# Squared row scale at the adds, sums of squares on ScalarE, and an earlier start of retention's q in a two-layer trunk

## The chip, the cores and the metric

The kernel runs on one core of one Trainium2 chip. The metric is the device time of one execution in microseconds (us). TensorE (PE) multiplies, VectorE (DVE), ScalarE (ACT) and GpSimd (POOL) do the elementwise work, SyncE (SP) issues DMAs. SBUF is the on-chip memory with 128 partitions, and PSUM holds eight banks of 128x512 f32 into which TensorE accumulates.

## The reference, cut to what matters

A sequence of 512 tokens with width 1024 passes through two layers, each a token mixer and a squared-ReLU MLP of hidden width 4096, and then a final norm. All is float32.

```python
def rms_norm(x, g):                      # over the width of 1024
    return x * lax.rsqrt(jnp.mean(x * x, -1, keepdims=True) + 1e-6) * g

def squared_relu_mlp(h, w_up, w_down):
    u = jax.nn.relu(h @ w_up)            # 1024 -> 4096
    return (u * u) @ w_down              # 4096 -> 1024

h = x
h = h + stick_breaking_attention(rms_norm(h, g_mix[0]), ...)   # 16 heads of 64
h = h + squared_relu_mlp(rms_norm(h, g_mlp[0]), ...)           # "MLP0"
h = h + retention(rms_norm(h, g_mix[1]), ...)                  # 4 heads
h = h + squared_relu_mlp(rms_norm(h, g_mlp[1]), ...)           # "MLP1"
return rms_norm(h, g_final)
```

The row factor r of a norm is positive, one number for each token. So relu(r·z)² = r²·relu(z)², and r² can stand behind the second product of the MLP as well.

## The kernel before, in words

**Layout.** The state h lies transposed, as eight tiles of 128 features by 512 tokens (`h[0]` to `h[7]`). Each operand of a product is split into a rounded part hi (a cast, by ScalarE) and the rest lo (a subtraction, by VectorE), and each product is made of three 128x512 matmuls, hi·hi, hi·lo and lo·hi. A helper records each TensorE instruction behind the one before it, so TensorE runs in the order in which the code is written; a scheduler orders the other engines, by priorities that it draws from the program, and each engine then works through its own list strictly in order. All matmuls have line L79 and all transposes L82, all splits of made operands L109 (hi) and L110 (lo).

**Weights.** `load_w` fetches 128 rows of two k-tiles, casts them (L119) and subtracts in two halves of 128x512 (L122, tile `wlo`).

**Norms.** A `Norm` sums squares of h over the features: ScalarE squares (L221), VectorE adds (`ssum`), `begin` and `end` sum over partitions by 16 narrow matmuls (`ss`), and GpSimd takes the power to r. `broadcast` builds a diagonal of r on VectorE (`diag`, L256) and multiplies it by ones (`rbps`) to have r along the free axis, as `rb`. The gain is multiplied in when x, the split input of the next product, is made from h (`next_x`: xhi on ScalarE, xlo on VectorE).

**MLP.** `mlp_s` makes eight groups of up products (96 matmuls into four banks each; the bank sets are `set_a`, four banks of tag "a", and `set_b`, two of "z" and two of "t"). At a group's end VectorE makes u = max(up, 0)·rb (L586) and ScalarE squares it into U (L587). Each pair of groups gives a chunk of the down product, which is formed with seven block products of 24 matmuls instead of eight (`plan`; sums of blocks are formed in S and B by VectorE, L639 to L650). `prep` splits a block's operands (tiles a and b, each in halves 0 and 1) one product ahead. Up groups of later chunks and down products alternate on TensorE, 9 matmuls by 6, then 18 matmuls of down. Behind each block product `add_up` adds its two banks to hT, the output laid out by tokens (L726; the first touch in MLP0 is a copy by ScalarE, L723). The last of the four chunks has no up group beside it; its plan is X, Z, X, Z, Y, X, V, by the names of their banks, and V is the last product of an MLP.

**Ends.** At the end of MLP0 hT is transposed back, feature tile by feature tile (`back`, bank `dT`), added to h (L274), and split into x, and retention starts: `side_by_side` makes the first head's q in two banks, x4 to x7 first. At the end of MLP1 the final norm follows: VectorE takes statistics of hT (`stats`, L775; L794 to L797), multiplies the right half by the gain (`scaled`, L779), GpSimd takes the power (L799), ScalarE scales the right half (L801) and VectorE the left (L804), and both halves go out by DMA. Rows 0 and 1 are worked off behind the Y product, rows 2 and 3 behind X and V. The core of it is

```python
for b in blocks:                      # tokens_out(0, 1) after Y, tokens_out(2, 3) after V
    ...
    nc.vector.bn_aggr(mv, sums[b].rearrange("p j s -> p (j s)"))
    ...
    nc.gpsimd.tensor_tensor(r, ms, mhalf[:, 0:1], op=ALU.pow)
    ...
    nc.scalar.activation(o, o, AF.Copy, scale=r)
    ...
    nc.vector.scalar_tensor_tensor(o, o, r, gf[0][:, left], op0=ALU.mult, op1=ALU.mult)
```

Of the kernel before, what the change touches and what calls it, by code (L numbers as in the profile page):

```python
# [12 lines left out]
P = 128  # L13
D = 1024
# [10 lines left out]
def trunk_kernel(  # L25
# [86 lines left out]
    def load_w(src, a, b, name, home=None, sub=None):  # L112

        pool, bufs = home or (wp, 3)
        raw = wp.tile([P, a, b], F32, tag="raw", name=f"raw_{name}", bufs=3)
        nc.sync.dma_start(raw, src)
        hi = pool.tile([P, a, b], F32R, tag="whi", name=f"whi_{name}", bufs=bufs)
        lo = pool.tile([P, a, b], F32R, tag="wlo", name=f"wlo_{name}", bufs=bufs)
        nc.scalar.copy(hi, raw)  # L119
        for j in range(min(a, 2)):  # L120
            ks = slice(j * a // 2, (j + 1) * a // 2) if a > 1 else slice(0, 1)
            (sub or nc.vector).tensor_tensor(  # L122
                lo[:, ks, :], raw[:, ks, :], hi[:, ks, :].bitcast(F32), op=ALU.subtract
            )
        return hi, lo
# [137 lines left out]
    def next_x(k, g, norm):  # L263

        gk = gain[:, g, k : k + 1]
        xhi, xlo = x[k]
        nc.scalar.activation(xhi, h[k], AF.Copy, scale=gk)
        nc.vector.scalar_tensor_tensor(
            xlo, h[k], gk, xhi.bitcast(F32), op0=ALU.mult, op1=ALU.subtract
        )  # L270
        norm.add(k)
# [265 lines left out]
    def mlp_s(layer, norm, finish=None):  # L537
# [13 lines left out]
        with ExitStack() as st:  # L551
            mp = st.enter_context(tc.tile_pool(name=f"mlp{layer}", bufs=2, reuse_waits="tile"))
            hT = mp.tile([P, NB, D], F32, name="hT", bufs=1)
            rb = None
# [10 lines left out]
            def up_steps(g, tags):  # L565

                nonlocal rb
# [16 lines left out]
                for m in range(4):  # L584
                    u = mp.tile([P, S], F32, tag="u", name=f"u{layer}_{g}_{m}")
                    nc.vector.scalar_tensor_tensor(u, banks[m], 0.0, rb, op0=ALU.max, op1=ALU.mult)  # L586
                    nc.scalar.activation(U[:, m, :], u, AF.Square)  # L587
# [128 lines left out]
            def add_up(acc, blocks):  # L716
                for half, cols, sign in blocks:
                    new = finish and (half, cols.start) not in begun
                    begun.add((half, cols.start))
                    for b in range(2):  # L720
                        at = hT[:, 2 * half + b, cols]
                        if new:
                            nc.scalar.activation(at, acc[b], AF.Copy, scale=float(sign))  # L723
                        else:
                            op = ALU.add if sign > 0 else ALU.subtract
                            nc.vector.tensor_tensor(at, at, acc[b], op=op)  # L726

            def down_steps(c):
                ch, banks = chunks[c], {}
                ending = c == CH - 1  # L730
                tags = {"X": "z", "Z": "t", "Y": "a" if ending else "t", "V": "a"}
                order = last_order if ending else range(7)
                for at, (name, blocks) in enumerate(last_plan if ending else plan):
# [20 lines left out]
            def behind(n):

                if finish:
                    back(4 + n, "zt"[n % 2])
                elif n == 0:
                    for b in (2, 3):
                        stats(b, 1)  # L760
                        scaled(b, 1)

            def back(d, tag):
                t = bank(f"dT{layer}_{d}", tag)
# [3 lines left out]
                finish(d)  # L768

            sums = {}  # L770

            def stats(b, j):
                if b not in sums:
                    sums[b] = small.tile([P, 2, 6], F32, tag=f"fst{b}", name=f"fst6_{b}", bufs=1)
                nc.vector.bn_stats(sums[b][:, j, :], hT[:, b, (left, right)[j]])  # L775

            def scaled(b, j):
                at = hT[:, b, (left, right)[j]]
                nc.vector.tensor_tensor(at, at, gf[0][:, (left, right)[j]], op=ALU.mult)  # L779

            def tokens_out(*blocks):

                if finish:
                    if blocks[0]:
                        for d in range(4):
                            back(d, "zt"[d % 2])
                    return
                for b in blocks:
                    if b < 2:
                        stats(b, 1)  # L790
                        scaled(b, 1)
                    stats(b, 0)
                    mv = small.tile([P, 2], F32, tag="mv", name=f"fmv_{b}")
                    nc.vector.bn_aggr(mv, sums[b].rearrange("p j s -> p (j s)"))  # L794
                    ms = small.tile([P, 1], F32, tag="ve", name=f"fms_{b}")
                    nc.vector.tensor_tensor(ms, mv[:, 0:1], mv[:, 0:1], op=ALU.mult)
                    nc.vector.scalar_tensor_tensor(ms, mv[:, 1:2], EPS, ms, op0=ALU.add, op1=ALU.add)  # L797
                    r = small.tile([P, 1], F32, tag="rstd", name=f"fr_{b}")
                    nc.gpsimd.tensor_tensor(r, ms, mhalf[:, 0:1], op=ALU.pow)  # L799
                    o = hT[:, b, right]  # L800
                    nc.scalar.activation(o, o, AF.Copy, scale=r)  # L801
                    nc.scalar.dma_start(out[b * P : (b + 1) * P, right], o)
                    o = hT[:, b, left]
                    nc.vector.scalar_tensor_tensor(o, o, r, gf[0][:, left], op0=ALU.mult, op1=ALU.mult)  # L804
                    nc.sync.dma_start(out[b * P : (b + 1) * P, left], o)
# [24 lines left out]
    def ret_layer(norm0, norm1):  # L830
        w = w_ret_in
        with ExitStack() as st:
# [5 lines left out]
            def side_by_side(c0, name):  # L838

                order = (4, 5, 6, 7, 0, 1, 2, 3)  # L840
                o = [bank(f"{name}{j}", "a") for j in (1, 2)]
                ws = [w_cols(w, 0, c0 + j * P, f"{name}{j}_0") for j in range(2)]
                for ks in (order[:4], order[4:6], order[6:]):
                    for j in range(2):
                        for k in ks:
                            whi, wlo = ws[j]
                            yield from mm3_steps(
                                o[j], whi[:, k, :], wlo[:, k, :], *x[k], k == order[0], k == order[-1]
                            )
                return o  # L850
# [97 lines left out]
            for hd in range(RET_HEADS):  # L948
                dec = rp.tile([P, S], F32, tag="dec", name=f"dec{hd}", bufs=1)
                nc.scalar.dma_start(dec, decay[:, hd, :])  # L950
                qs = ahead or Steps(rotated_steps(hd * 256, f"q{hd}"))
                ahead = None
# [9 lines left out]
                k = whole(rotated_steps(D + hd * 256, f"k{hd}"))  # L962
# [110 lines left out]
```

## Time and profile before

| | |
|---|---|
| three runs | median 1355.61 us (1354.31 to 1355.77) |
| the profiled execution | 1354.56 us, span 1352.8 us, granted TensorE clock 0.996 |
| start to 253.5 us | attention; PE busy 248.7 us, DVE 196.8 us |
| 253.5 to 594.6 us | MLP0; PE 335.4 us, DVE 243.3 us, ACT 149.8 us |
| 594.6 to 994.0 us | retention; PE 398.8 us, DVE 223.7 us |
| 994.0 to 1290.0 us | MLP1 with up groups; PE 296.0 us, DVE 197.7 us |
| 1290.0 to 1330.0 us | MLP1, last chunk; PE 38.4 us, DVE 39.8 us |
| 1330.0 us to the end | V, final norm, output; PE 7.7 us, DVE 16.6 us |

Times inside an execution are counted from the start of its span. In a row of the timeline stand start, duration, engine, line, operation, output<-inputs and shapes, then the number of instructions joined in the row, and in brackets the time that the engine was idle before it with what ended that. A row's duration is longer than the distance to the next start, since instructions of one engine overlap a little: two 128x512 matmuls start 0.227 us apart and each lasts 0.39 us.

### The profile page before, as it was taken

The page shows a single profiled execution, that of the slowest core. Times are in us where ns is not written, and L with a number is a line of the kernel's source. Part 1 is how long each engine was busy: PE and PEld are TensorE (multiplying, and loading weights), DVE is VectorE, ACT ScalarE, POOL GpSimd, SP SyncE. Part 2 cuts the span into 40 slices and gives each one's busy share as a digit, 9 for nine tenths or more (in the row PEclk, how much of TensorE's full clock was granted, in tenths as well). Part 3 has the DMA queues.
Part 4 walks back from the last instruction along what each step waited for, and adds up shares of the span by engine and source line. Part 5 has one row for each costly group of instructions (what it writes and reads, how often), then busy time and mean ns, then how long its engine had stood idle before and what let it go on. Part 6 is the DMA issues. An engine that isn't in the chain of part 4 may idle for free.

```text
span 1352.8 us, 16109 instructions
## 1 busy us (share of the span) xinstructions
PE 1324.9 (98%) x6082; PEld 1095.6 (81%) x6082; DVE 917.9 (68%) x1345; ACT 573.2 (42%) x824; POOL 116.5 (9%) x142
## 2 busy tenths in 40 slices
PE   9999999999999999989999999999999999999995
PEld 7888888788888888778888888888888888888874
DVE  5788886846586775986565554555574668667598
ACT  6466654534444443543332322322253344444352
POOL 1000000200111111100000000000110011111110
PEclk9999999999999999999999999999999999999998
DMA  6455442543454455413232232232434344544351
GB/s 205 125 149 124 120 122 79 163 117 94 143 130 133 113 128 162 83 52 109 71 94 86 78 94 86 78 95 77 159 106 125 83 151 110 140 125 110 109 105 67
DMA packets 99086, 152.13 MB, mean 112 GB/s; under 512 B 5952, under 2 KB 42944, under 8 KB 99008
## 3 DMA queue, kind: packets, MB, share of 16 engines
q1 hardware_dynamic: 79648, 98.12, 24.2%
q0 software_dynamic: 17920, 50.34, 15.3%
q10 hardware_dynamic: 1440, 2.64, 0.5%
q8 instruction: 48, 0.79, 0.2%
q14 instruction: 30, 0.25, 0.1%
HBM read 138.49 MB, written 2.10 MB: 104 GB/s over the span
## 4 chain that ended last, share of the span: by engine, by line
PE 51%; DVE 3%; issue 1%; POOL 0%; ACT 0%; DVEq 0%; POOLq 0%
PE up L79 13%; PE rout L79 7%; PE rg L79 6%; PE rv L79 6%; PE X L79 5%; PE k L79 3%; PE Z L79 3%; PE q L79 2%; PE ro L79 2%; PE Y L79 1%; PE rs L79 1%; DVE hT L726 1%; PE yt L82 1%; DVE fst L775 0%; DVE b_1lo L110 0%
## 5 line engine op out<-in xcount | busy, mean ns | idle before, releaser
L79 PE MATMUL up<-xhi,wlo_up 128*128 128x512 f32 x512 | 200.4, 391 | 0.9 <-DVE wlo_up L122 0.9
L79 PE MATMUL up<-xhi,whi_up 128*128 128x512 f32 x512 | 200.6, 392 | 0.0
L79 PE MATMUL up<-xlo,whi_up 128*128 128x512 f32 x512 | 200.3, 391 | 0.0
L602 POOL DMA_DIRECT2D B<-in_w_mlp_down x92 | 82.8, 903 | 562.3 <-DVE b_1lo L110 261.3
L122 DVE TENSOR_TENSOR wlo_up<-raw_up,whi_up 128x512 fp32r<-128x512 f32 x128 | 83.8, 686 | 66.6 <-ACT whi_up L119 66.6
L79 PEld LDWEIGHTS up<-xhi,wlo_up 128*128 128x128 f32 x512 | 96.1, 188 | 22.0 <-DVE wlo_up L122 1.4
L79 PEld LDWEIGHTS up<-xlo,whi_up 128*128 128x128 f32 x512 | 96.7, 189 | 20.8 <-issue 0.5
L79 PEld LDWEIGHTS up<-xhi,whi_up 128*128 128x128 f32 x512 | 96.1, 188 | 19.7
L119 ACT CAST whi_up<-raw_up 128x1024 fp32r<-128x1024 f32 x64 | 67.1, 1049 | 99.0 <-PE up L79 83.7
L110 DVE TENSOR_TENSOR b_0lo<-B,b_0hi 128x1024 fp32r<-128x1024 f32 x56 | 68.4, 1221 | 3.6 <-ACT b_0hi L109 1.2
L110 DVE TENSOR_TENSOR b_1lo<-B,b_1hi 128x1024 fp32r<-128x1024 f32 x56 | 68.3, 1220 | 2.1 <-ACT b_1hi L109 2.1
L587 ACT ACTIVATE U<-u 128x512 f32<-128x512 f32 x64 | 38.8, 628 | 62.6 <-DVE u L586 61.8
L109 ACT CAST b_0hi<-B 128x1024 fp32r<-128x1024 f32 x56 | 58.7, 1048 | 13.5 <-DVE B L644 5.2
L109 ACT CAST b_1hi<-B 128x1024 fp32r<-128x1024 f32 x56 | 58.7, 1048 | 7.9 <-DVE B L644 3.5
L586 DVE SCALAR_TENSOR_TENSOR u<-up,rb_n 128x512 f32<-128x512 f32 x64 | 42.9, 688 | 27.0 <-PE up L79 26.3
L79 PE MATMUL rout<-ylo,whi_rout 128*128 128x512 f32 x128 | 51.0, 399 | 0.0
L79 PE MATMUL rout<-yhi,wlo_rout 128*128 128x512 f32 x128 | 51.0, 398 | 0.0
L79 PE MATMUL q<-xlo,whi_q 128*128 128x512 f32 x128 | 50.8, 397 | 0.0
L79 PE MATMUL q<-xhi,wlo_q 128*128 128x512 f32 x128 | 50.6, 395 | 0.0
L79 PE MATMUL rout<-yhi,whi_rout 128*128 128x512 f32 x128 | 50.5, 395 | 0.0
L79 PE MATMUL k<-xlo,whi_k 128*128 128x512 f32 x128 | 50.4, 394 | 0.0
L79 PE MATMUL q<-xhi,whi_q 128*128 128x512 f32 x128 | 50.2, 392 | 0.0
(290 smaller groups left out, 3254.2 us busy)
## 6 DMA issues: line engine op xcount, KB each, us to landing
B<-in_w_mlp_down POOLq DMA_DIRECT2D x96, 512.0 KB, 5.4
raw_up<-in_w_mlp_up SPq DMA_DIRECT2D x64, 512.0 KB, 3.7
raw_rv<-in_w_ret_in SPq DMA_DIRECT2D x16, 512.0 KB, 3.8
raw_rg<-in_w_ret_in SPq DMA_DIRECT2D x16, 512.0 KB, 3.6
raw_rout<-in_w_ret_out SPq DMA_DIRECT2D x16, 512.0 KB, 3.6
raw_q<-in_w_sb_in SPq DMA_DIRECT2D x8, 512.0 KB, 4.6
raw_k<-in_w_sb_in SPq DMA_DIRECT2D x8, 512.0 KB, 4.0
q<-hi SPq DMA_DIRECT2D x32, 128.0 KB, 3.6
```

Source lines behind the costliest of these rows:

```text
L79: pe(nc.tensor.matmul(o, a, b, start=start, stop=stop, **kw))
L82: pe(nc.tensor.transpose(o, a, ident))
L109: nc.scalar.copy(hi, src_ap)
L110: (eng or nc.vector).tensor_tensor(lo, src_ap, hi.bitcast(F32), op=ALU.subtract)
L119: nc.scalar.copy(hi, raw)
L122: (sub or nc.vector).tensor_tensor(lo[:, ks, :], raw[:, ks, :], hi[:, ks, :].bitcast(F32), op=ALU.subtract)
L586: nc.vector.scalar_tensor_tensor(u, banks[m], 0.0, rb, op0=ALU.max, op1=ALU.mult)
L587: nc.scalar.activation(U[:, m, :], u, AF.Square)
L602: nc.gpsimd.dma_start(t[:, ks, :], src[:, ks, :], **kw)
L726: nc.vector.tensor_tensor(at, at, acc[b], op=op)
```

## The change

The change has six parts.

1. `load_w` subtracts in one operation of 128x1024.
2. The MLPs' norm has no broadcast. r² and −r² are made by two small VectorE operations, `norm.begin` and `norm.end` stand after 48 matmuls of the first group instead of 28, and at a group's end ScalarE takes relu from PSUM to U and then squares U in place. The relus and squares are 64 each over both MLPs.
3. `add_up` multiplies by r² or −r², a number for each partition, while it adds (one VectorE operation as before, of another form; the first touch in MLP0 stays with ScalarE).
4. In the last chunk the banks of X and Z change tags.
5. MLP0's end: V's transposes stand late in V, then 24 matmuls of retention's q on x4 to x7 (`early`) ahead of the transposes of x0 to x3, and the norm's sums behind all of these. In retention the norm and its broadcast stand 20 and 30 matmuls into k.
6. MLP1's end: sums of squares by ScalarE with its accumulator (`squares`), the gain's multiplication by GpSimd (`by_gain`, L807 in the new numbering), two small VectorE operations (L811, L812), the power by GpSimd (L814), and the row multiplications as before (L819, L822).

```diff
-        for j in range(min(a, 2)):
-            ...
+        (sub or nc.vector).tensor_tensor(lo, raw, hi.bitcast(F32), op=ALU.subtract)
...
-                    if g == 0 and n == 28:
+                    if g == 0 and n == 48:
                         norm.begin()
                         r = norm.end()
-                    if g == 0 and n == 52:
-                        rb = norm.broadcast(r)
+                        nc.vector.tensor_tensor(r2[:, 0, :], r, r, op=ALU.mult)
+                        nc.vector.tensor_scalar(r2[:, 1, :], r2[:, 0, :], -1.0, None, op0=ALU.mult)
...
                 for m in range(4):
-                    u = mp.tile([P, S], F32, tag="u", name=f"u{layer}_{g}_{m}")
-                    nc.vector.scalar_tensor_tensor(u, banks[m], 0.0, rb, op0=ALU.max, op1=ALU.mult)
-                    nc.scalar.activation(U[:, m, :], u, AF.Square)
+                    nc.scalar.activation(U[:, m, :], banks[m], AF.Relu)
+                for m in range(4):
+                    nc.scalar.activation(U[:, m, :], U[:, m, :], AF.Square)
...
-                            op = ALU.add if sign > 0 else ALU.subtract
-                            nc.vector.tensor_tensor(at, at, acc[b], op=op)
+                            nc.vector.scalar_tensor_tensor(at, acc[b], by, at, op0=ALU.mult, op1=ALU.add)
...
-                tags = {"X": "z", "Z": "t", "Y": "a" if ending else "t", "V": "a"}
+                tags = {"X": "t", "Z": "z", "Y": "a", "V": "a"} if ending else {"X": "z", "Z": "t", "Y": "t"}
...
+            def between(at, n):
                 if finish:
-                    back(4 + n, "zt"[n % 2])
+                    if at == 6 and n >= 14 and (n - 14) % 3 == 0:
+                        back(4 + (n - 14) // 3)
+                elif at == 4 and n == 3:       # Y: squares(0, 1), squares(1, 1), by_gain(0), by_gain(1)
+                elif at == 5 and n == 15:      # X: squares(0, 0), squares(1, 0), row_scale(0), row_scale(1)
+                elif at == 6 and n == 3:       # V: squares and by_gain of 2 and 3, rows_out(0), rows_out(1)
...
+            def back_left(acc, blocks):
+                add_up(acc, blocks)
+                early.go(24)
+                for d in x_order[4:]:
+                    back(d)
+                for d in x_order:
+                    nxt.add(d)
...
+            def squares(b, j):
+                junk = mp.tile([P, 512], F32, tag="junk", name=f"junk{b}_{j}", bufs=1)
+                nc.scalar.activation(junk, hT[:, b, (left, right)[j]], AF.Square, accum_out=ssq[:, b, j : j + 1])
+            def by_gain(b):
+                at = hT[:, b, right]
+                nc.gpsimd.tensor_tensor(at, at, gf[0][:, right], op=ALU.mult)
...
+            def last_out(acc, blocks):
+                add_up(acc, blocks, (0,))
+                squares(2, 0)
+                row_scale(2)
+                add_up(acc, blocks, (1,))
+                squares(3, 0)
+                rows_out(2)
+                row_scale(3)
+                rows_out(3)
...
-                    qs.go(40)
+                    qs.go(24)
+                    ks.go(20)
                     norm0.begin()
                     r = norm0.end()
-                    qs.go(7)
+                    ks.go(10)
                     rb = norm0.broadcast(r)
```

VectorE in MLP1's last chunk, from the Y adds to the lo of V's operands. Before (a1_3_6 and b1_3_6 are V's operands, the last digit is the half; gf is the gain, fr the row factor):

```order
L726 TENSOR_TENSOR hT_8218<-hT_8218,Y1_3_1_10623 128x512
L775 BN_STATS fst6_0_10668<-hT_8218 128x6 x2
L779 TENSOR_TENSOR hT_8218<-hT_8218,gf_10618 128x512
L794 BN_AGGR fmv_0_10672<-fst6_0_10668 128x2
L775 BN_STATS fst6_1_10683<-hT_8218 128x6
...
L804 SCALAR_TENSOR_TENSOR hT_8218<-hT_8218,fr_0_10677,gf_10618 128x512
...
L110 TENSOR_TENSOR b1_3_6_0lo_10705<-B1_3_00_10380,b1_3_6_0hi_10704 128x1024
...
L804 SCALAR_TENSOR_TENSOR hT_8218<-hT_8218,fr_1_10692,gf_10618 128x512
L110 TENSOR_TENSOR b1_3_6_1lo_10725<-B1_3_00_10380,b1_3_6_1hi_10724 128x1024
```

The same place now:

```order
L110 TENSOR_TENSOR b1_3_4_1lo_10445<-B1_3_01_10169,b1_3_4_1hi_10444 128x1024
L728 SCALAR_TENSOR_TENSOR hT_8073<-Y1_3_0_10408,r2_8074,hT_8073 128x512
L110 TENSOR_TENSOR a1_3_4_1lo_10441<-U1_6_9866,a1_3_4_1hi_10440 128x512
L728 SCALAR_TENSOR_TENSOR hT_8073<-Y1_3_1_10409,r2_8074,hT_8073 128x512
L110 TENSOR_TENSOR a1_3_6_0lo_10463<-U1_7_10153,a1_3_6_0hi_10462 128x512
L110 TENSOR_TENSOR b1_3_6_0lo_10467<-B1_3_00_10166,b1_3_6_0hi_10466 128x1024
L110 TENSOR_TENSOR a1_3_6_1lo_10483<-U1_7_10153,a1_3_6_1hi_10482 128x512
L110 TENSOR_TENSOR b1_3_6_1lo_10487<-B1_3_00_10166,b1_3_6_1hi_10486 128x1024
L811 TENSOR_TENSOR fms_0_10496<-ssq1_8075 128x1
```

The statistics, the gain and the row multiplications of rows 0 and 1 no longer stand between the Y adds and V's operands; the row multiplications now follow the X adds.

GpSimd at the same place, now (before there are only the four powers behind the last DMA):

```order
L603 DMA B1_3_00_10166<-in_w_mlp_down 128x2x512 x2
L807 TENSOR_TENSOR hT_8073<-hT_8073,gf_10404 128x512 x2
L814 TENSOR_TENSOR fr_0_10499<-fms_0_10496,mhalf_74 128x1
L814 TENSOR_TENSOR fr_1_10504<-fms_1_10501,mhalf_74 128x1
L807 TENSOR_TENSOR hT_8073<-hT_8073,gf_10404 128x512 x2
L814 TENSOR_TENSOR fr_2_10564<-fms_2_10561,mhalf_74 128x1
L814 TENSOR_TENSOR fr_3_10576<-fms_3_10573,mhalf_74 128x1
```

Four multiplications by the gain have come to GpSimd, behind its last DMA.

TensorE in V at the end of MLP0, before:

```order
L79 MATMUL V_3_0_5048<-b_3_6_0hi,a_3_6_0hi 128x512
L82 MATMUL dT_4_5054<-ident,hT 128x128 x4
L79 MATMUL V_3_0_5048<-b_3_6_0lo,a_3_6_0hi 128x512
...
L82 MATMUL dT_7_5103<-ident,hT 128x128 x4
L79 MATMUL V_3_1_5049<-b_3_6_1lo,a_3_6_1hi 128x512
L79 MATMUL V_3_1_5049<-b_3_6_1hi,a_3_6_1lo 128x512
L82 MATMUL dT_0_5118<-ident,hT 128x128 x4
```

and now:

```order
L79 MATMUL V_3_1_4968<-b_3_6_0hi,a_3_6_0lo 128x512
L82 MATMUL dT_4_4984<-ident,hT 128x128 x4
...
L79 MATMUL V_3_1_4968<-b_3_6_1hi,a_3_6_1lo 128x512
L82 MATMUL dT_7_5017<-ident,hT 128x128 x4
L79 MATMUL q_5027<-xhi_94,whi_q_0_5031 128x512
L79 MATMUL q_5027<-xlo_95,whi_q_0_5031 128x512
L79 MATMUL q_5027<-xhi_94,wlo_q_0_5032 128x512
L79 MATMUL q_5027<-xhi_96,whi_q_0_5031 128x512
```

The transposes of x4 to x7 stood after 4, 10, 16 and 22 of V's 24 matmuls and stand after 15, 18, 21 and 24, and q's first matmuls come directly behind them.

VectorE at that place, now (h4 and xlo4 belong to x4, and so on):

```order
L273 TENSOR_TENSOR h4_82<-dT0_4_4984,h4_82 128x512
L120 TENSOR_TENSOR wlo_k01_0_5156<-raw_k01_0_5153,whi_k01_0_5155 128x1024
L264 SCALAR_TENSOR_TENSOR xlo4_95<-h4_82,gain_71,xhi4_94 128x512
L273 TENSOR_TENSOR h5_83<-dT0_5_4995,h5_83 128x512
L273 TENSOR_TENSOR h6_84<-dT0_6_5006,h6_84 128x512
L273 TENSOR_TENSOR h7_85<-dT0_7_5017,h7_85 128x512
L264 SCALAR_TENSOR_TENSOR xlo5_97<-h5_83,gain_71,xhi5_96 128x512
```

The whole lo of a weight and the adds of h6 and h7 stand between the adds of h4 and h5 and the lo of x5.

More of the change, by code (lines that the diff above doesn't have):

```diff
@@ L261, in broadcast, with scaled_x @@
             return rb
[L263 removed]
+    def scaled_x(k, g):
         gk = gain[:, g, k : k + 1]
@@ L270, in next_x @@
         )
+    def next_x(k, g, norm):
+        scaled_x(k, g)
         norm.add(k)
@@ L714, in mlp_s, with add_up @@
             begun = set()
-            def add_up(acc, blocks):
+            def add_up(acc, blocks, only=(0, 1)):
                 for half, cols, sign in blocks:
                     new = finish and (half, cols.start) not in begun
-                    begun.add((half, cols.start))
-                    for b in range(2):
-                        at = hT[:, 2 * half + b, cols]
+                    if only[-1] == 1:
+                        begun.add((half, cols.start))
+                    for b in only:
+                        t = 2 * half + b
+                        at, by = hT[:, t, cols], r2[:, int(sign < 0), t : t + 1]
                         if new:
-                            nc.scalar.activation(at, acc[b], AF.Copy, scale=float(sign))
+                            nc.scalar.activation(at, acc[b], AF.Copy, scale=by)
                         else:
-                            op = ALU.add if sign > 0 else ALU.subtract
-                            nc.vector.tensor_tensor(at, at, acc[b], op=op)
+                            nc.vector.scalar_tensor_tensor(at, acc[b], by, at, op0=ALU.mult, op1=ALU.add)
             def down_steps(c):
@@ L767, in back @@
                 residual(d, t)
[L768 to L805, printed above, removed]
@@ new lines, in rows_out @@
+            def rows_out(b):
+                rows, r = slice(b * P, (b + 1) * P), scales[b]
+                o = hT[:, b, left]
+                nc.vector.scalar_tensor_tensor(o, o, r, gf[0][:, left], op0=ALU.mult, op1=ALU.mult)
+                nc.sync.dma_start(out[rows, left], o)
+                o = hT[:, b, right]
+                nc.scalar.activation(o, o, AF.Copy, scale=r)
+                nc.scalar.dma_start(out[rows, right], o)
+            def last_out(acc, blocks):
[7 more added lines that the diff above has]
+                rows_out(3)
@@ L827, in mlp_s, with side_by_side, ret_layer @@
                 dn.end()
-    def ret_layer(norm0, norm1):
+    x_order = (4, 5, 6, 7, 0, 1, 2, 3)
+    def side_by_side():
+        o = [bank(f"q0{j}", "a") for j in (1, 2)]
+        ws = [w_cols(w_ret_in, 0, j * P, f"q0{j}_0") for j in range(2)]
+        for ks in (x_order[:4], x_order[4:6], x_order[6:]):
+            for j in range(2):
+                for k in ks:
+                    whi, wlo = ws[j]
+                    yield from mm3_steps(
+                        o[j], whi[:, k, :], wlo[:, k, :], *x[k], k == x_order[0], k == x_order[-1]
+                    )
+        return o
+    def ret_layer(norm0, norm1, early):
         w = w_ret_in
@@ L836, in ret_layer @@
             crs = rp.tile([P, 2, S], F32, name="crs", bufs=1)
[L838 to L850, printed above, removed]
             def rotated_steps(c0, name):
                 if name == "q0":
-                    t1, t2 = yield from side_by_side(c0, name)
+                    while not early.done:
+                        early.go(1)
+                        yield
+                    t1, t2 = early.value
                 else:
@@ L961, in ret_layer @@
                 q = qs.end()
-                k = whole(rotated_steps(D + hd * 256, f"k{hd}"))
+                k = ks.end()
                 v = values(hd, group(w, 2 * D + hd * RV, KT, x, f"rv{hd}", set_b, token_major=True))
```

59 lines of the change are left out of this document (39 added, 20 removed).

## The prediction

> **What bounds the kernel.** I read the page's busy times first, then what TensorE waited for, then the places of the longest waits on the timeline.
>
> ```profile
> span 1352.8 us, 16109 instructions
> PE 1324.9 (98%) x6082; PEld 1095.6 (81%) x6082; DVE 917.9 (68%) x1345; ACT 573.2 (42%) x824; POOL 116.5 (9%) x142
> ```
>
> TensorE is busy for 1324.9 of 1352.8 us, so work taken from other engines is worth nothing unless TensorE waits for it. Gains can come from matmuls removed, from the 28 us of gaps, and from the tail. The waits of TensorE (total, times, longest):
>
> ```profile
> PE V L79 <- DVE b_0lo L110: 4.8, 1, 4.8
> PE dT L82 <- DVE hT L726: 3.2, 2, 2.5
> PE X L79 <- DVE hT L726: 2.1, 2, 1.1
> PE X L79 <- DVE b_1lo L110: 1.1, 2, 0.6
> PE up L79 <- DVE wlo_up L122: 0.9, 1, 0.9
> ```
>
> All lie at the ends of the MLPs or the start of one, the largest in front of V in MLP1. Matmuls there, and a table by stretches (length, busy PE, PEld, DVE, ACT, POOL, then the granted clock):
>
> ```profile
> 1330.10 0.39 PE L79 MATMUL V<-b_0hi,a_0hi 128*128 128x512 f32 x1
> 1335.33 0.80 PE L79 MATMUL V<-b_0lo,a_0hi 128*128 128x512 f32 x1 [4.84 <-DVE b_0lo L110]
> 1300.00:1310.00 10.00, 10.00 (x46) 8.14 (x45) 10.00 (x14) 4.58 (x6) 2.44 (x2) 1.00 0.34 55
> 1335.00:1338.00 3.00, 2.67 (x6) 1.82 (x6) 2.56 (x5) 0.72 (x1) 0.87 (x1) 0.54 0.22 83
> ```
>
> V's second matmul waits 4.84 us, and after that pause the clock is 0.54 for a while. In the last chunk VectorE is full (10.00 of 10.00) and as late as TensorE. VectorE's list there:
>
> ```profile
> 1295.60 1.27 DVE L726 TENSOR_TENSOR hT<-hT,X 128x512 f32<-128x512 f32 x2
> 1296.79 0.69 DVE L110 TENSOR_TENSOR a_0lo<-S,a_0hi 128x512 fp32r<-128x512 f32 x1
> 1297.39 1.22 DVE L110 TENSOR_TENSOR b_0lo<-B,b_0hi 128x1024 fp32r<-128x1024 f32 x1
> 1298.53 0.68 DVE L639 TENSOR_TENSOR S<-U,U 128x512 f32<-128x512 f32 x1
> ...
> 1306.29 1.23 DVE L110 TENSOR_TENSOR b_0lo<-B,b_0hi 128x1024 fp32r<-128x1024 f32 x1
> ...
> 1327.12 1.28 DVE L726 TENSOR_TENSOR hT<-hT,Y 128x512 f32<-128x512 f32 x2
> 1328.32 1.28 DVE L775 BATCH_NORM_STATS2 fst<-hT 128x6 f32<-128x512 f32 x2
> ...
> 1334.06 1.22 DVE L110 TENSOR_TENSOR b_0lo<-B,b_0hi 128x1024 fp32r<-128x1024 f32 x1
> ...
> 1336.39 0.75 DVE L804 SCALAR_TENSOR_TENSOR hT<-hT,fr,gf 128x512 f32<-128x512 f32 x1 [0.44 <-POOL fr L799]
> 1337.06 1.22 DVE L110 TENSOR_TENSOR b_1lo<-B,b_1hi 128x1024 fp32r<-128x1024 f32 x1
> ...
> 1346.67 1.42 DVE L804 SCALAR_TENSOR_TENSOR hT<-hT,fr,gf 128x512 f32<-128x512 f32 x2 [0.59 <-POOL fr L799]
> ```
>
> From start to start an add or a subtraction of 128x512 takes 0.60 us (1296.79 to 1297.39), one of 128x1024 1.14 us (to 1298.53), and the form with a number for each partition 0.67 us (1336.39 to 1337.06). From 1328.32 to the lo of V's operand stands the norm of rows 0 and 1. The last VectorE operation ends at 1348.09, and 4.7 us of output follow.
>
> **The parts and their costs.** The sum is made against the profiled execution, 1354.56 us; the median of the runs is 1.05 us above it.
>
> Broadcast in the MLPs. The chain of waits has, in MLP1,
>
> ```profile
> 1012.77 0.86 PE rbps_n L79 x2
> ```
>
> It is TensorE's own work in a stretch without gaps, and it goes in both MLPs: −1.7 us. The norm's sums only move, and r² isn't wanted before the first add.
>
> Relu and square. Per group VectorE loses four u of 0.67 us, and ScalarE has eight operations instead of four.
>
> ```profile
> L587 ACT ACTIVATE U<-u 128x512 f32<-128x512 f32 x64 | 38.8, 628 | 62.6 <-DVE u L586 61.8
> 1289.52 0.40 PE L79 MATMUL up<-xhi,wlo_up 128*128 128x512 f32 x1
> ```
>
> At 0.6 us each, with the two casts that its new list has between them, the four relus are through about 1.9 us after the last up matmul (1289.52), and the banks are wanted after 24 matmuls of down, 24 × 0.227 = 5.4 us. ScalarE waited 61.8 us for u in all. I take 0; bounds 0 and +1.4 (0.1 us at each of 14 group ends, should a cast come late). VectorE's relief is covered by TensorE everywhere but in the last chunk.
>
> Whole lo of a weight. Only at the start of MLP0 does TensorE wait for one:
>
> ```profile
> 254.27 1.28 DVE L122 TENSOR_TENSOR wlo_up<-raw_up,whi_up 128x512 fp32r<-128x512 f32 x2
> 255.01 0.50 PE L79 MATMUL up<-xhi,wlo_up 128*128 128x512 f32 x1 [0.92 <-DVE wlo_up L122]
> ```
>
> The first half was enough there; now the whole is waited for, 1.14 − 0.60 = +0.5 us. Elsewhere weights come ahead and the 0.5 us are hidden.
>
> Last chunk up to V. Against VectorE's list before I go through the new one: two u leave (−1.3 us), but one U subtraction comes earlier (+0.6), S waits for the last two squares (about +0.6), and adds cost 0.07 us more each (eleven, +0.8). So VectorE has the lo of the third product's first operand at about 1307.8 instead of 1307.4, TensorE, which starts the chunk 1.1 us sooner because X has free banks (half of the 2.1 us above), waits 1.3 and 1.0 us in the third product, and V starts at about 1330.5 instead of 1330.1: +0.4 us in MLP1 and, with both U subtractions and a weight's lo in the list, +0.7 us in MLP0. Bounds −1.1 (banks alone) to +2.
>
> V and the tail of MLP1. With these lengths the new list, which has no gap from the third product on, reaches the end of the Y adds at 1328.3, as before. With the norm of rows 0 and 1 out of the way, the lo of V's first half follows directly: 1328.3 + 0.60 + 1.14 = 1330.0, so V does not wait, and the lo of the second half is there at 1331.8, where V wants it. V ends 24 × 0.227 later, at 1336.2 instead of 1342.7, at full clock. VectorE: X adds to 1334.7, two row multiplications to 1336.0, V adds to 1337.4. Then the chain of the last rows, by these groups:
>
> ```profile
> L221 ACT ACTIVATE sq_n<-h 128x512 f32<-128x512 f32 x28 | 17.3, 617 | 0.0
> L799 POOL TENSOR_TENSOR fr<-fms,mhalf 128x1 f32<-128x1 f32 x4 | 2.8, 704 | 31.8 <-DVE fms L797 31.8
> ```
>
> The square by ScalarE, behind a row scale in its queue, ends at 1337.9; then come two small operations (0.3), the power (0.7), a row multiplication (0.67), and the same small chain for row 3, which stands behind that multiplication: 1341.5 against 1348.1, −6.6 us.
>
> But four multiplications by the gain now run on GpSimd beside it, of which before shows the like only in the attention:
>
> ```profile
> 194.77 1.60 POOL L110 TENSOR_TENSOR o<-oF,o 128x512 fp32r<-128x512 f32 x1 [13.05 <-ACT o L109]
> 195.40 1.52 DVE L423 TENSOR_TENSOR sg<-sg,keep 128x511 f32<-128x511 f32 x1
> L110 POOL TENSOR_TENSOR o<-oF,o 128x512 fp32r<-128x512 f32 x7 | 9.7, 1388 | 176.4 <-ACT o L109 176.4
> ```
>
> A VectorE operation with both inputs in SBUF, which takes 0.68 us alone, took 1.52 us beside it: +0.84. The first two multiplications fall on the casts b of X and V (two SBUF inputs), the third on the row multiplications, the fourth on V adds, whose one input is in PSUM. Three by 0.84 = 2.5 us, of which 0.4 lie in the wait for ScalarE: gain 6.6 − 2.1 = −4.5 us. Bounds −6.6 (none counts) and −3.1 (1.30 each). I take 0.84, since it is the price that a row shows.
>
> The Trainium skill, *SBUF — State Buffer*, section *Who interferes with whom*, says that such a pair contends for one shared port pair, which whoever issues first holds for its whole instruction; the trace agrees as far as the VectorE operation of 195.40 ends 0.55 us after GpSimd's does (194.77 + 1.60 = 196.37). Where GpSimd comes first from the start, the price by this rule is a whole GpSimd operation.
>
> End of MLP0 and start of retention. TensorE from V's start to the first matmul of rv:
>
> ```profile
> 581.99 0.39 PE L79 MATMUL V<-b_0hi,a_0hi 128*128 128x512 f32 x1
> 585.61 0.66 PE L82 MATMUL dT<-ident,hT 128*128 128x128 f32 x4 [2.54 <-DVE hT L726]
> 593.19 1.64 PE L82 MATMUL dT<-ident,hT 128*128 128x128 f32 x13 [0.65 <-DVE hT L726]
> 608.00 1.10 PE L79 MATMUL rbps_n<-diag_n,ones 128*128 128x512 f32 x2 [0.63 <-DVE diag_n L256]
> 620.05 0.39 PE L79 MATMUL rv<-whi_rv,xhi 128*128 128x512 f32 x1
> ```
>
> Of 38.1 us 3.8 are waits (2.54 + 0.65 + 0.63); the rest, the same matmuls, stays. The first wait shrinks to some 0.3, as the transposes come 11 × 0.227 = 2.5 us later; the second goes, as 24 matmuls (5.4 us) stand between V and dT0; the third goes, as ten matmuls (2.3 us) instead of seven stand in front of the broadcast. What is late next is x. Between the add of h4 and the lo of x5 VectorE has 1.14 + 0.67 + 3 × 0.60 us, and q wants x5 three matmuls after x4: about 1.4 us of wait, 0.3 more for x6, and for x0 to x3, whose adds, casts and lo start with dT0, about 1.3. Sum 3.3: −0.5 us; bounds −3.8 (x in time) and +1.5.
>
> Sum: −1.7 + 0.5 + 0.7 − 0.5 − 4.5 = −5.5 (the +0.4 of MLP1 stands in the tail's times). That is 1349.1 us in the frame of the profiled execution and 1350.1 from the median. A profiled execution need not lie as far under the median the next time; I take the middle, **1349.6 us**.
>
> **Rivals.** (1) GpSimd's multiplications cost VectorE nothing: the last operation ends at 1341.5, 2.1 us more are gained, 1347.5 us. For it: most rows of GpSimd (mean 1388 ns) ran beside VectorE without a trace of it; against it the row of 195.40.
> (2) Each of the three costs a whole operation of 1.30 us: 3 × 0.46 = 1.4 us less, 1351.0 us. For it, VectorE's list is unbroken there, so a GpSimd operation that gets in is in front of a whole VectorE operation. By the rule of the Trainium skill above (*SBUF — State Buffer*, *Who interferes with whom*) this price is the one paid.
> (3) x is in time in retention: 3.3 us more, 1346.3 us. The long list between h4 and x5 speaks against it.
> (4) The change does not do in the tail what it says: V waits as long as before, now for a cast that ScalarE makes late, because its list has two squares between the casts of X's and V's operands. Then only −1.7 + 0.5 remain with small terms, 1354.5 us, no change. For it, a square with accumulator has no row; one would have to cost 2 us more than the 0.6 us of a plain one.
> (5) Slower: ScalarE at the ends of the groups. If the eight operations and the casts behind them made TensorE wait there, with 14 ends in two MLPs, it would decide from (5.5 + 2.7)/14 = 0.6 us each. At 0.9 us each it gives 1349.6 + 12.6 = 1362 us. Against it, the 3.5 us between relus done and banks wanted.
>
> **How the numbers follow.** Chances: forecast 0.40, (1) 0.20, (2) 0.16, (3) 0.06, (4) 0.12, (5) 0.06. About 0.2% (2.7 us) is what a measurement can tell from no change, so faster begins under 1352.9: forecast, (1), (2) and (3), 0.82. Same is (4), 0.12; slower is (5), 0.06. The range leaves out (4) and (5), 0.18 in all, and takes in the ends of the other terms: 1345.2 below (rival 3 and no lost start), 1353.0 above (rival 2 with +2 in the last chunk).
>
> **What would show it.** Right: no rbps in the MLPs; V in MLP1 at 0.23 us a matmul with waits under 1 us; last VectorE operation at 1342 to 1345 on the clock of before less the 1 to 2 us gained earlier; casts b of 128x1024 that take about 2 us beside GpSimd's multiplications; a wait of about 1 us for xlo in q. Wrong: a wait for up banks at groups' ends, V still waiting 3 us or more, or TensorE waits of several us in the last chunk, which VectorE's list, counted here by hand, would then have caused.

## The result: 0.5% faster, and the profile after

| | before | changed |
|---|---|---|
| runs, median | 1355.69 us (1354.31 to 1356.12, 4 runs) | 1348.28 us (1348.08 to 1350.28, 4 runs) |
| the profiled execution, its span | 1354.56, 1352.8 us | 1350.28, 1348.5 us |

The ratio is 0.995, 95% interval 0.9933 to 0.9968. Forecast were 1349.6 us. The page's first lines of the changed kernel:

```profile
span 1348.5 us, 15871 instructions
PE 1325.7 (98%) x6078; PEld 1093.8 (81%) x6078; DVE 867.5 (64%) x1121; ACT 607.8 (45%) x902; POOL 124.5 (9%) x146
```

VectorE lost 50 us of work and ScalarE gained 35; TensorE is as busy as before. What TensorE waits for now (total, times, longest), the small waits in the attention left out:

```profile
PE X L79 <- DVE hT L728: 1.8, 3, 0.6
PE X L79 <- DVE b_0lo L110: 1.5, 2, 0.8
PE q L79 <- DVE xlo L264: 1.5, 3, 0.6
PE up L79 <- DVE wlo_up L120: 1.5, 1, 1.5
...
PE X L79 <- DVE b_1lo L110: 1.1, 2, 0.5
...
PE X L79 <- ACT b_0hi L109: 0.6, 1, 0.6
...
PE q L79 <- ACT xhi L263: 0.2, 1, 0.2
```

The 4.8 us in front of V are gone, and so are the waits of the transposes, of the broadcast, and of X for its banks at the start of the last chunks. In their place stand q's waits for x, a longer one for the first weight's lo, and three of X for its banks in the mixed stretches, where the kernel before has none. V and the end, on TensorE, VectorE, GpSimd and ScalarE:

```profile
1331.55 0.39 PE L79 MATMUL V<-b_0hi,a_0hi 128*128 128x512 f32 x1
1337.39 0.39 PE L79 MATMUL V<-b_1hi,a_1lo 128*128 128x512 f32 x1
1326.01 1.22 DVE L110 TENSOR_TENSOR b_1lo<-B,b_1hi 128x1024 fp32r<-128x1024 f32 x1
1327.91 1.03 DVE L110 TENSOR_TENSOR a_1lo<-U,a_1hi 128x512 fp32r<-128x512 f32 x1
1329.53 1.13 DVE L110 TENSOR_TENSOR a_0lo<-U,a_0hi 128x512 fp32r<-128x512 f32 x1
1336.35 1.02 DVE L819 SCALAR_TENSOR_TENSOR hT<-hT,fr,gf 128x512 f32<-128x512 f32 x1
1337.30 1.76 DVE L819 SCALAR_TENSOR_TENSOR hT<-hT,fr,gf 128x512 f32<-128x512 f32 x1
1343.31 0.75 DVE L819 SCALAR_TENSOR_TENSOR hT<-hT,fr,gf 128x512 f32<-128x512 f32 x1 [0.72 <-POOL fr L814]
1323.95 4.44 POOL L807 TENSOR_TENSOR hT<-hT,gf 128x512 f32<-128x512 f32 x1 [10.14 <-ACT junk L801]
1328.36 1.74 POOL L807 TENSOR_TENSOR hT<-hT,gf 128x512 f32<-128x512 f32 x1
1335.54 1.28 POOL L807 TENSOR_TENSOR hT<-hT,gf 128x512 f32<-128x512 f32 x1
1336.79 1.72 POOL L807 TENSOR_TENSOR hT<-hT,gf 128x512 f32<-128x512 f32 x1
1339.75 0.63 ACT L801 ACTIVATE junk<-hT 128x512 f32<-128x512 f32 x1 [2.72 <-DVE hT L728]
1340.29 0.19 ACT L801 ACTIVATION_READ_ACCUMULATOR junk<-hT 128x1 f32 x1
```

V's 24 matmuls start within 5.84 us instead of 12.16. The four multiplications by the gain take GpSimd 4.44, 1.74, 1.28 and 1.72 us. On VectorE the subtractions of 128x1024 (lo of b) still take 1.22 us beside the first of them; two of 128x512 (lo of a) take 1.03 and 1.13 instead of 0.68, and two row multiplications 1.02 and 1.76 where two took 1.42 together. Each of these four longer operations ends 0.55 to 0.56 us after a GpSimd multiplication ends (1328.39, 1330.10, 1336.82 and 1338.51).

To say where the time went, I cut both profiled executions at TensorE's first and last instructions of each stage (us):

| stretch of TensorE | before | changed | difference |
|---|---|---|---|
| start to first up of MLP0 | 253.46 | 255.43 | +1.97 |
| first up to first X: MLP0; MLP1 | 49.54; 52.20 | 49.20; 51.28 | −0.34; −0.92 |
| first X to last up (mixed): MLP0; MLP1 | 238.39; 238.39 | 237.95; 238.87 | −0.44; +0.48 |
| last up to V (last chunk): MLP0; MLP1 | 40.60; 40.58 | 41.32; 40.72 | +0.72; +0.14 |
| V of MLP0 to first rv | 38.06 | 36.97 | −1.09 |
| rv to first up of MLP1 | 378.88 | 379.81 | +0.93 |
| V of MLP1, its starts; from there to the end | 12.16; 10.54 | 5.84; 11.11 | −6.32; +0.57 |

The sum is −4.3, the difference of the spans. The 1.97 us at the start are no part of the change: in that execution the first matmuls ran slowly, in others of the same program text there (the kernel without GpSimd's multiplications, below) not. A row of the changed kernel:

```profile
6.96 0.63 PE L79 MATMUL v<-whi_v,xlo 128*128 128x512 f32 x1
```

and the same matmul of that kernel:

```profile
6.41 0.40 PE L79 MATMUL v<-whi_v,xlo 128*128 128x512 f32 x1
```

The profiled execution of the changed kernel is 2.0 us above its median, that of before 1.1 below: −4.3 − 2.0 − 1.1 = −7.4, the difference of the medians.

### The profile page after: what moved, and what is told of

It is laid out like the page before. It is cut to its first block, busy times and chain, and to the rows that moved or that the text cites. A ratio compares the mean times of both kernels' runs of the same rounds, so it can differ in the third digit from the quotient of the medians.

```text
span 1348.5 us, 15871 instructions
## 1 busy us (share of the span) xinstructions
PE 1325.7 (98%) x6078; PEld 1093.8 (81%) x6078; DVE 867.5 (64%) x1121; ACT 607.8 (45%) x902; POOL 124.5 (9%) x146
## 4 chain that ended last, share of the span: by engine, by line
PE 91%; DVE 6%; issue 1%; ACT 1%; DMA 0%; POOLq 0%; POOL 0%; DVEq 0%
PE up L79 25%; PE X L79 9%; PE rout L79 7%; PE rg L79 7%; PE k L79 6%; PE rv L79 6%; PE q L79 6%; PE Z L79 5%; PE v L79 3%; PE Y L79 3%; PE so L79 3%; PE ro L79 2%; PE z L79 2%; PE av L79 1%; PE t L82 1%
## 5 line engine op out<-in xcount | busy, mean ns | idle before, releaser
L120 DVE TENSOR_TENSOR wlo_up<-raw_up,whi_up 128x1024 fp32r<-128x1024 f32 x64 | 78.1, 1222 | 79.0 <-ACT whi_up L119 79.0
L109 ACT CAST b_0hi<-B 128x1024 fp32r<-128x1024 f32 x56 | 58.7, 1048 | 4.0 <-PE X L79 2.1
L586 ACT ACTIVATE U<-up 128x512 f32<-128x512 f32 x64 | 37.1, 592 | 49.1 <-PE up L79 49.1
L79 PE MATMUL k<-xhi,whi_k 128*128 128x512 f32 x128 | 50.4, 394 | 0.0
L79 PE MATMUL rg<-whi_rg,xhi 128*128 128x512 f32 x128 | 50.2, 392 | 0.0
```

The costliest lines, as they stand in the source:

```text
L79: pe(nc.tensor.matmul(o, a, b, start=start, stop=stop, **kw))
L109: nc.scalar.copy(hi, src_ap)
L120: (sub or nc.vector).tensor_tensor(lo, raw, hi.bitcast(F32), op=ALU.subtract)
L586: nc.scalar.activation(U[:, m, :], banks[m], AF.Relu)
```

## The experiments

They were run in three groups, each beside the kernel before on the same chip: e1, e2, e10 and e6 (median of before 1355.83 us), e16, e11, e13 and e14 (1356.05), and e17 to e20 (1354.78). Ratios are to the kernel before of the same group.

**The tail alone (e1).** In the kernel before, only the final norm is exchanged for the new one:

```diff
-                    if ending and at == 4:
-                        tokens_out(0, 1)
...
+                elif at == 4 and n == 3:       # squares, by_gain, row_scale, rows_out and last_out as in part 6
```

> The kernel before with part 6 alone (the new final norm). Theory T (the gain is made in MLP1's tail, because the final norm's VectorE work leaves the place in front of V's casts and shrinks): V's wait of 4.84 us goes, VectorE ends 4 to 5.5 us earlier, about 1350.5 us. Rival S (the gain is spread, VectorE needs the relief of relu and of whole lo as well): V still waits 2 us or more, 1353 us or later.

Measured: 1357.64 us, ratio 1.0011 (1.0002 to 1.002). Slower, and yet V's wait went as expected:

```profile
PE V L79 <- DVE b_0lo L110: 0.2, 1, 0.2
```

From V's first matmul to the end it takes 16.6 us instead of 22.7. The time was lost where nothing had been changed: each MLP's mixed stretch took 241.28 and 241.27 us instead of 238.39, without a wait.

**The tail undone (e2).** In the changed kernel the old final norm is put back.

```diff
-                elif at == 4 and n == 3:       # and the rest of part 6
                 elif at == 6 and n == 3:
                     for b in (2, 3):
+                        stats(b, 1)
+                        scaled(b, 1)
...
+                    if ending and at == 4 and not finish:
+                        tokens_out(0, 1)
```

> The changed kernel with part 6 undone (final norm as before, parts 1 to 5 kept). T: V waits 4 to 5 us again and some 5.5 us are lost, about 1353.8 us. Rival S: at most 2 us are lost, 1349 to 1350.3 us.

Measured: 1361.92 us, ratio 1.0045 (1.0031 to 1.0059), slower than before. V waits again,

```profile
PE V L79 <- DVE b_0lo L110: 4.3, 1, 4.3
```

and from V to the end it takes 23.9 us instead of the changed kernel's 17.0: 6.9 us, somewhat more than the 5.5 of T. The rest is again in the mixed stretches (242.29 and 242.97 us). Neither theory had a place for that.

**The place of the norm alone (e10).**

```diff
+                        if ending and at == 6 and n == 13:
+                            tokens_out(0, 1)
                         yield
...
-                    if ending and at == 4:
-                        tokens_out(0, 1)
```

> The kernel before with one thing moved: the final norm of rows 0 and 1, still on VectorE, stands in V instead of ahead of it. Theory E (what counts is that VectorE has less to do up to the end): V's wait goes, but the same 13 us of VectorE work stand behind the X adds, the last operation ends at about 1347.5, 1355.1 us. Rival P (what counts is the place alone, V's wait and the clock after it): the whole gain of about 5 us, 1350.7 us.

Measured: 1355.49 us, ratio 0.9996 (0.9987 to 1.0005): E. V is through in 5.58 us, but 16.7 us follow instead of 10.5. With V's wait gone VectorE's list is still there. So it is not enough to take the norm out of V's way; work had to leave VectorE's list. Which of the two that left counts more, the sums of squares or the gain, no run separates.

**Without GpSimd's multiplications (e6).**

```diff
-                nc.gpsimd.tensor_tensor(at, at, gf[0][:, right], op=ALU.mult)
+                pass
```

> The changed kernel with GpSimd's four multiplications by the gain left out: the right half of the output is not multiplied by g_final. Theory L (they hold up VectorE's operations with two SBUF inputs): the two lo of 1.03 and 1.13 us go back to 0.68, the two row multiplications from 2.71 us to 1.42, about 2 us in all on VectorE, of which 1.2 at least on the path, 1346.3 to 1347.1 us. Rival 1 of the prediction (they cost VectorE nothing on the path): 1348.3 us.

Measured: 1346.06 us, ratio to before 0.9929 (0.9917 to 0.9942), 2.2 us under the changed kernel. The same operations on VectorE there:

```profile
1327.18 0.68 DVE L110 TENSOR_TENSOR a_0lo<-U,a_0hi 128x512 fp32r<-128x512 f32 x1
1333.55 1.41 DVE L819 SCALAR_TENSOR_TENSOR hT<-hT,fr,gf 128x512 f32<-128x512 f32 x2
```

L it is, by 0.2 us more than its range. V takes 5.2 us instead of 5.8, and what follows 9.7 instead of 11.1.

**What made e1 and e2 slow? (e16)** The same matmuls took 1.2 to 1.9% longer in a stretch nearly without waits. The compiled programs show what else differs: the new small tiles ssq and r2 take 32 bytes in each partition, and every tile allocated behind them starts elsewhere. In before the tiles of the MLPs (U, B, a, b, S) start at 960 modulo 1024 bytes, in e2 at 992. In e1 they start at 800, since the tiles of the old norm's statistics go as well. In the changed kernel both shifts together give 832, while retention's tiles, which stand ahead of r2 and move with ssq alone, start at 800.

> The kernel before with a tile of 32 bytes that nothing reads put ahead of the others in the pool of small tiles, so that every later tile (norms, attention's, both MLPs', retention's) starts 32 bytes further on; no other instruction changes. Theory A (tiles that start 32 bytes off a multiple of 64 make TensorE's matmuls beside them slower, as the two slow kernels' up and down matmuls of 0.230 us instead of 0.227 suggest): +2.9 us in each MLP and +0.9 us in retention, 1362.5 us or more. Rival N (it was something else in those two kernels): 1355.7 us.

```diff
+    pad = small.tile([P, 8], F32, tag="pad", name="pad", bufs=1)
+    nc.gpsimd.memset(pad, 0.0)
```

Measured: 1363.78 us, ratio 1.006 (1.0048 to 1.0073). So the place of the tiles costs time, as A has it; whether its rule of 64 bytes holds is the next question. The mixed stretch of MLP0 and retention, as the table by windows has them (length, busy PE with its count, PEld, DVE, ACT, POOL, granted clock), of before and of this kernel:

```profile
303.00:541.39 238.39, 238.39 (x1048) 196.91 (x1047) 160.65 (x214) 102.32 (x135) 31.02 (x36) 1.00 0.47 128
620.05:998.93 378.88, 378.88 (x1721) 313.57 (x1720) 207.19 (x356) 115.74 (x150) 12.40 (x21) 1.00 0.31 94
```

```profile
302.93:544.57 241.64, 241.64 (x1048) 196.32 (x1046) 160.95 (x214) 102.17 (x135) 31.00 (x36) 1.00 0.46 127
624.81:1005.17 380.36, 380.36 (x1722) 313.42 (x1720) 207.18 (x356) 115.75 (x150) 12.36 (x21) 1.00 0.30 94
```

The same 1048 matmuls, the same work on the other engines, TensorE busy all the time and the clock at 1.00: 3.25 us longer, for a tile that nothing reads. It isn't only the matmuls that read the moved tiles: two up matmuls, which read x and weights alone, and these lie where they lay, start 0.231 us apart on average in this stretch instead of 0.227.

**The parts with tiles of 64 bytes (e11, e13, e14).** The edits, beside parts of the change (e11 is part 6 alone, e13 parts 2 and 3, e14 the whole change):

```diff
-            ssq = small.tile([P, NB, 2], F32, tag="ssq", name=f"ssq{layer}", bufs=1)
+            ssq = small.tile([P, NB, 4], F32, tag="ssq", name=f"ssq{layer}", bufs=1)
-            r2 = mp.tile([P, 2, NB], F32, name="r2", bufs=1)
+            r2 = mp.tile([P, 4, NB], F32, name="r2", bufs=1)
```

> The kernel before with part 6 alone, as e1_tail_alone, but the new small tile ssq takes 64 bytes instead of 32, so that the tiles behind it start at multiples of 64 again. A: the MLPs run at 0.227 us a matmul, and the tail's gain of about 5 us shows: 1351 us. N: 1357.6 us as without it.

> The kernel before with parts 2 and 3 alone (relu and square on ScalarE, r squared at the adds), the tile r2 taking 64 bytes. A, with the broadcast's 0.86 us gone from each MLP and a last chunk that gains little: 1354.0 to 1354.6 us. Rival S (relief of VectorE is what the change lives on): 1352 us or less.

> The changed kernel with ssq and r2 of 64 bytes each instead of 32 (in the changed kernel the two together leave the MLPs' tiles at multiples of 64, but retention's 32 off). A: retention is 0.9 us shorter, 1347.4 us. N: 1348.3 us.

Measured: 1344.79 us for the tail alone (ratio 0.9919, 0.9906 to 0.9933), 1360.23 for parts 2 and 3 (1.0036, 1.0023 to 1.0049), 1349.88 for the changed kernel (0.9958, 0.9945 to 0.9972). The first was 6 us better than forecast, the second 6 worse, the third 2.5 worse; so a multiple of 64 is not the rule. Their MLP tiles start at 832, 0 and 896 modulo 1024, with mixed stretches of 237.10, 240.69 and 240.91 us in MLP0. Parts 2 and 3 alone can't be judged by their time; but the stretch ahead of the first X, where no such difference was seen, is 0.87 us shorter in MLP0 and 0.91 in MLP1, which is the broadcast.

**Separating the place from the change (e17 to e20).** In the kernel before `pad` as above, with `[P, 224]` (e17) or `[P, 32]` (e18); in the changed kernel (e19, e20) ssq as above and

```diff
-            r2 = mp.tile([P, 2, NB], F32, name="r2", bufs=1)
+            r2 = mp.tile([P, 64, NB], F32, name="r2", bufs=1)
```

> The kernel before with an unused tile of 896 bytes ahead in the pool of small tiles; the tiles of the mixers and MLPs then start at 832 modulo 1024, as in e11_tail_alone_64, instead of 960. Theory A (TensorE's rate in the stages depends on where these tiles lie): 1.3 us less in each MLP, 2.3 less in retention, 0.8 less in attention, 1350.2 us; then part 6 is worth the 5.4 us that are left of the 11.3 of e11. Rival N (e11's gain is part 6's own): 1355.9 us.

> The kernel before with an unused tile of 128 bytes ahead: the tiles start at 64 modulo 1024. Theory M (what counts is the start modulo 128: the quick places so far, 960 and 832, lie 64 off a multiple of 128, as x and the weights do, the slow ones, 992, 800, 896 and 0, do not): as before, 1355 to 1356.5 us. Rival Q (another pattern): 1358 us or more, or 1353.5 or less.

> The changed kernel with ssq of 64 bytes and r2 of 1024 bytes, so that the tiles of all stages start at 832 modulo 1024 (in the changed kernel attention's and retention's start at 800). A: retention 376.6 us instead of 379.8, attention 0.8 less, the MLPs unchanged, 1344.3 us. Rival N: 1348.3 us.

> As e19_after_832, and part 1 undone (lo of weights in two halves) and, in the last norm, the two row factors of a pair made in one operation each and the row multiplications of rows 0 and 1 put behind the V adds. The wait for the first weight's lo falls from 1.5 to 0.9 us; V's adds come 2.5 us earlier, and row 3's factor no longer stands behind row 2's multiplication: the last VectorE operation 2 us earlier; 1341.7 us in all. Rival (the scheduler's order and GpSimd's multiplications eat it): 1344 us.

Measured: 1350.20 us for before with 896 bytes (ratio 0.9965, 0.9953 to 0.9978), 1350.30 with 128 bytes (0.9965, 0.9952 to 0.9977), 1345.14 for the changed kernel at 832 throughout (0.9926, 0.9912 to 0.9939), 1342.18 for the last (0.9903, 0.9889 to 0.9916). The first came out as A had it. In the second M missed and Q holds: 64 is not as 960, it is better, as good as 832. In the third retention came to 376.53 us, as A had it. The windows of e17:

```profile
302.29:539.38 237.09, 237.09 (x1047) 196.39 (x1046) 160.33 (x214) 102.32 (x135) 31.04 (x36) 1.00 0.47 129
619.66:996.20 376.54, 376.54 (x1721) 313.33 (x1720) 207.04 (x356) 115.75 (x149) 12.39 (x21) 1.00 0.30 95
```

| starts modulo 1024: MLPs; retention | program | mixed stretch of MLP0; MLP1 | rv to up |
|---|---|---|---|
| 960; 960 | before | 238.39; 238.39 | 378.88 |
| 992; 992 | before (e16) | 241.64; 241.64 | 380.36 |
| 832; 832 | before (e17) | 237.09; 237.09 | 376.54 |
| 64; 64 | before (e18) | 237.09; 237.09 | 376.56 |
| 800; 800 | part 6 alone (e1) | 241.27; 241.27 | 379.81 |
| 832; 832 | part 6 alone (e11) | 237.09; 237.09 | 376.56 |
| 0; 960 | parts 2 and 3 (e13) | 240.69; 240.88 | 378.89 |
| 992; 960 | changed without part 6 (e2) | 242.29; 242.97 | 378.80 |
| 832; 800 | changed | 237.95; 238.87 | 379.81 |
| 896; 832 | changed (e14) | 240.91; 241.65 | 376.56 |
| 832; 832 | changed (e19) | 237.99; 238.83 | 376.53 |

Each stretch goes by the place of its own stage's tiles: retention takes 378.8 to 378.9 us at 960 in three programs and 376.5 to 376.6 at 832 in four, whatever the MLPs' tiles do.

So at a like place part 6 is worth about 5 us: 5.4 by the medians of e17 and e11 (1350.20 and 1344.79, from two groups whose medians of before lie 1.3 us apart), and 4.7 in the stretches that it touches, since V to the end takes 6.1 us less but the last chunk ahead of V 1.4 us more (42.05 instead of 40.63). Parts 1 to 5 together bring nothing (1344.79 to 1345.14), but they are gains and losses that cancel. From e11 to e19 the broadcasts and the first lo give 1.3 us, the end of MLP0 1.1 and the last chunk of MLP1 1.3, while that of MLP0 loses 1.0 and the mixed stretches 2.6. Of these parts only part 1 is tried by itself, by undoing it in e20, and parts 2 and 3 as a pair in e13; parts 4 and 5 are read from their stretches alone.

The last kernel, e20, is the fastest of all, 6.1 us under the changed one. Its edits beside the place: lo in halves again, and

```diff
+                ms = small.tile([P, 2], F32, tag="ve", name=f"fms_{b}")
+                nc.vector.tensor_tensor(ms, ssq[:, b : b + 2, 0], ssq[:, b : b + 2, 1], op=ALU.add)
...
+                add_up(acc, blocks, (1,))
+                squares(3, 0)
+                row_scale(2)
+                for b in range(NB):
+                    rows_out(b)
```

The 3.0 us against e19 are near the 2.6 forecast, from other places: in the profiled executions the tail from V to the end gives 1.0 us where 2 were expected, and the mixed stretches 1.7 where none was. With the halves the three waits of X for its banks have all but gone. The first of them in e19, and the same place in e20 (L732 is the add there):

```profile
464.68 1.22 DVE L120 TENSOR_TENSOR wlo_up<-raw_up,whi_up 128x1024 fp32r<-128x1024 f32 x1
465.82 1.22 DVE L110 TENSOR_TENSOR b_1lo<-B,b_1hi 128x1024 fp32r<-128x1024 f32 x1
466.95 1.40 DVE L728 SCALAR_TENSOR_TENSOR hT<-X,r,hT 128x512 f32<-128x512 f32 x2
466.87 0.39 PE L79 MATMUL up<-xhi,wlo_up 128*128 128x512 f32 x1
467.85 0.47 PE L79 MATMUL X<-b_0hi,a_0hi 128*128 128x512 f32 x1 [0.59 <-DVE hT L728]
468.15 0.40 PE L79 MATMUL X<-b_0lo,a_0hi 128*128 128x512 f32 x1
```

```profile
463.61 0.68 DVE L122 TENSOR_TENSOR wlo_up<-raw_up,whi_up 128x512 fp32r<-128x512 f32 x1
464.21 1.22 DVE L110 TENSOR_TENSOR b_1lo<-B,b_1hi 128x1024 fp32r<-128x1024 f32 x1
465.34 1.40 DVE L732 SCALAR_TENSOR_TENSOR hT<-X,r,hT 128x512 f32<-128x512 f32 x2
465.79 0.39 PE L79 MATMUL up<-xhi,wlo_up 128*128 128x512 f32 x1
466.23 0.47 PE L79 MATMUL X<-b_0hi,a_0hi 128*128 128x512 f32 x1
466.54 0.39 PE L79 MATMUL X<-b_0lo,a_0hi 128*128 128x512 f32 x1
```

From the up matmul to the second X matmul it takes 1.28 us in e19 and 0.75 in e20, where two starts without a wait take 0.45. The 0.59 of the waits' list leaves out a part of this, since it counts idle time only from the end of the row before. At the end of e20 the row multiplications of rows 2 and 3:

```profile
1334.15 1.41 DVE L821 SCALAR_TENSOR_TENSOR hT<-hT,fr,gf 128x512 f32<-128x512 f32 x2 [0.81 <-POOL fr L815]
```

Rows 2 and 3 now share one wait for their factors.

## Why the prediction was right, and where its terms were off

The forecast was −5.5 us by the parts, and −7.4 were measured. The change also moves tiles, which the prediction did not know: −1.30 in each MLP (960 to 832) and +0.93 in retention (960 to 800), −1.7 us. At a like place (e17 to e19) the change brought −5.1. That this is so near the sum of the parts is in part luck: the mixed stretches lost 2.6 us that had been put at nothing, and the end of MLP0 and the tail together gave about 3 us more than forecast.

- Broadcast and whole lo, −1.7 + 0.5: measured −0.34 − 0.92 = −1.3 in the stretches ahead of X. The wait for the first lo is 1.46 instead of 0.92 us, +0.54.
- Relu and square 0, lo hidden elsewhere: this step failed. At a like place (e17 to e19) the mixed stretches grew by 0.90 and 1.74 us. Of these 2.6 us, 2.5 are the three waits of X for banks whose adds come late (hT, L728): listed with 0.59 us, each costs 0.83 from start to start (1.28 less 0.45 in the rows above). The wrong part is "hidden elsewhere": the whole lo of 1.22 us stands ahead of the adds in VectorE's list, and in halves again (e20) 1.7 of the 2.6 us went. The 0.3 us that are left at each of the three places are not explained. With the 0.5 at the first lo the whole lo lost 2.2 us.
- Last chunk, +0.7 and +0.4: +0.72 and +0.14.
- End of MLP0, −0.5: −1.1 in these executions. Waits of 0.60, 0.23, 0.60 and 0.30 us replaced 3.82; the 3.3 forecast were too many, x6 and x7 came in time, so rival 3 holds in part. The old code has two times here. In before and e11 it takes 38.1 us; in e1, e10, e16, e17 and e18 39.6 to 39.7, since the clock falls after the wait of 2.5 us (to 0.57 to 0.64 over the four us behind it; e10 is shown), although that wait is 2.52 to 2.54 us long in all seven and the clock stays at 1.00 in before and e11:

```profile
586.00:590.00 4.00, 4.00 (x15) 3.19 (x14) 2.97 (x6) 2.00 (x4) 0.00 (x0) 0.57 0.29 89
```

In six executions of the new code it took 36.9 to 37.1 us. So against the old code's more frequent time this part gains about 2.6 us.
- Tail: −4.9 from V's start (−4.5, and 0.4 of later start); measured −5.75. The list of VectorE was read right: V does not wait, the slow clock after that wait went, and VectorE's last operation ends 12.5 us after V's first matmul (1344.06 less 1331.55), where the forecast's times, 1330.5 and 1341.5 + 2.1, put 13.1.
- GpSimd, 2.1 us on the path: 2.2 measured by leaving it out (e6). So rivals 1 (nothing) and 2 (a whole operation each) fell. But the right sum is luck, since the split is another: not 0.84 us each at three operations, two of them casts b, but 0.35, 0.45, 0.28 and 1.02 at four, none of them a cast b. The Trainium skill (*SBUF — State Buffer*, *Who interferes with whom*) calls the shared port pair an exclusive lock and says that the order of issue decides who blocks. The trace agrees: each of the four VectorE operations ends 0.55 to 0.56 us after GpSimd's, as the row of 195.40 in the prediction did (in e20 a row multiplication ends 0.54 us after), and the first GpSimd multiplication, which starts inside a run of VectorE operations with two inputs in SBUF, takes 4.44 us instead of 1.39 while these keep their 1.22. What the prediction left out is that VectorE loses only what is left of GpSimd's operation when its own starts. That GpSimd gets in at the adds from PSUM, which stand in front of three of the four, fits the rows but is not tested.
- Rival 4 (V waits for ScalarE): no; a square with accumulator takes 0.63 us, and reading it 0.19. Rival 5 (ScalarE at the ends of the groups): TensorE waits for no up bank.

## What to carry to other kernels

Work moved off an engine counts where its list ends last: the final norm moved within VectorE's list brought nothing, and moved off the list about 5 us. One operation in place of two halves can lose: the whole lo saves VectorE time and delays what stands behind it. Before a small change is judged by a few us, look whether it moves tiles in SBUF, and compare stretches that it doesn't touch; a tile of unused bytes is a cheap control.

## What the runs showed of the hardware that was not expected

With the same instructions in the same order (but for the filling of the unused tile), TensorE's 1048 matmuls of a mixed stretch took 237.09, 238.39 or 241.64 us by where the other tiles start in SBUF (64 and 832, 960, 992 modulo 1024), 1.9% from best to worst, while the busy times of the other engines stayed within 0.4%. The up matmuls slow down with the others though they read only x and weights, so it is not, or not alone, the place of what a matmul reads. x and the weights lie at 64 modulo 256 in all of these kernels, and the quickest places, 64 and 832, are also 64 modulo 256; 960 is 192, 896 and 0 are not 64 modulo 128, and 992 and 800 are not multiples of 64. That the common phase is the cause is a guess: no run moved x or the weights, or one kind of tile of a stage alone.
